# Stores of h issued by ScalarE, a fourth raw weight buffer, and no accumulating DMA in the first four down passes, in a two-layer encoder trunk on one core

## The chip, the core and the metric

The kernel runs on one NeuronCore of a Trainium2 chip. Its engines work from queues of their own, each in order: TensorE (PE; PEld is its loading of stationary weights), VectorE (DVE), ScalarE (ACT), GpSimd (POOL) and SyncE (SP, which here only issues DMAs). The metric is the time of one execution on the device in microseconds (us). The median of three runs of the kernel before is 1787.04 us.

## What is computed

A trunk of two layers on 768 tokens of width 1024 (512 of one request, 256 of another; the weights are shared). All of it is float32.

```
for layer in 0, 1:
    h = rmsnorm(x, ln_mix)
    x = x + attention(h @ w_in) @ w_out      # layer 0: neighbourhood and grouped heads; layer 1: differential
    h = rmsnorm(x, ln_mlp[layer])
    x = x + square(relu(h @ w_up[layer])) @ w_down[layer]     # 1024 -> 4096 -> 1024
y = rmsnorm(x, ln_f)
```

The change touches the MLP, `square(relu(h @ w_up)) @ w_down`.

## The kernel before

**Number format.** TensorE multiplies values rounded to fp32r. To keep float32 accuracy every operand is split in two parts, hi (rounded) and lo (the rest), and every product is done as three matmuls, hi·hi, lo·hi and hi·lo. A weight therefore passes through three kinds of tile: `wraw` (as loaded by a DMA that SP issues, L84), `whi` and `wlo`. The split has two forms. `wsplit` (L86): ScalarE copies hi (L90), VectorE subtracts (L91, lo = raw − hi). `wsplit_acc` (L93): ScalarE copies hi (L95) and writes raw times −1, rounded like hi, into lo (L96), and POOL issues a DMA that reads the raw weights from memory a second time and adds them to lo (L97, "accumulating DMA").

**Stages of the MLP** (`mlp`, L1145), the same in both layers. The 4096 hidden features are done in groups. Four groups of 128 are done plainly (`up_plain`, `down`). The rest goes in pairs of groups through a Strassen-Winograd scheme: seven products in place of eight.

- Fourteen *up passes* (`up_fast`, L948). Each takes one weight matrix of 2 x 2 quarters and the tokens in two halves of 384 and does seven products, numbered 0 to 6 here, of 12 matmuls of 128 x 384 each: 0, 2, 4 and 6 add into the PSUM tile upx (X), 1 writes upy (Y), 3 and 5 write upz (Z). ScalarE and VectorE take the results out, square the positive part, and form the seven combinations that the down passes need, in a staging tile `hf` of seven parts (two such tiles). That tile is stored to DRAM as `h` (L998). The last two up passes keep plain values and store them in pieces (L1001).
- Fourteen *down passes* (`down_fast`, L1038), in the order of `PASSES`. Before a pass runs, `Forms.need` (L1017) loads the stored forms back (L1020) into `hf`, and ScalarE and VectorE split them into hi and lo (L1032, L1033). The seven products go to dnx, dny and dnz, and VectorE adds them to x (L1046).

**Weights of a pass** (`quarters`, L908). Two raw tiles A and B are loaded (L84). From them come four pairs of hi and lo: w1 (the quarters a11 and a12, used by products 0 and 1), w2 (products 3 and 4), w3 (products 2 and 5) and w4 (product 6). w2 comes from sums of quarters (L921). The hi and lo tiles have four slots each, so each of w1 to w4 has one slot from pass to pass: w1 of the next pass can be written only when product 1 (Y) of this pass has been done. Which quarters take the accumulating form is set by `acc`: (11,) in the up passes, that is the first half of w1; (11, 12) in the down passes, that is all of w1.

**Order.** The code is recorded and a scheduler sets the order of instructions on each engine ahead of time, by priority (the order of the code) and by its own estimate of when operands and buffers are free. So the number of buffers, and the engine that issues a DMA, move instructions on every engine. At run time each engine goes through its list in order.

Of the kernel before, what the change touches and what calls it, by code (L numbers as in the profile page):

```python
# [12 lines left out]
F32 = mybir.dt.float32  # L13
# [5 lines left out]
P = 128  # L19
# [4 lines left out]
NT = TS + TP  # L24
# [22 lines left out]
def kernel(ctx: ExitStack, tc: tile.TileContext, a: dict, y: bass.AP):  # L47
    nc = tc.nc
# [4 lines left out]
    rpool = ctx.enter_context(tc.tile_pool(name="rpool", bufs=1, side="right"))  # L53
# [23 lines left out]
    def wload(src, width, pieces=1):  # L77

        off = woff.get(src, 0)
        woff[src] = off + P * width  # L80
        raw = rpool.tile([P, 1024], F32, tag="wraw", name="wraw", bufs=3)[:, :width]
        view = a[src][off : off + P * width].rearrange("(p w) -> p w", w=width)
        w = width // pieces
        return raw, [lambda s=slice(i * w, (i + 1) * w): nc.sync.dma_start(raw[:, s], view[:, s]) for i in range(pieces)]  # L84
# [8 lines left out]
    def wsplit_acc(hi, lo, raw, src):  # L93

        nc.scalar.activation(hi, raw, AF.Copy)  # L95
        nc.scalar.activation(lo, raw, AF.Copy, scale=-1.0)  # L96
        nc.gpsimd.dma_start(lo, src, accum_op=ALU.add)  # L97

    def whilo(width):
        return (wpool.tile([P, 1024], F32R, tag="whi", name="whi", bufs=4)[:, :width],  # L100
                wpool.tile([P, 1024], F32R, tag="wlo", name="wlo", bufs=4)[:, :width])
# [801 lines left out]
    def staging(mp):  # L903
        return mp.tile([P, 7, NH], F32, tag="hf", name="hf", bufs=2)
# [3 lines left out]
    def quarters(src, n, mp, acc):  # L908

        off = woff[src]  # L910
        dA, dB = (a[src][o : o + P * 2 * n].rearrange("(p w) -> p w", w=2 * n) for o in (off, off + P * 2 * n))
        A, loads = wload(src, 2 * n)
        loads[0]()
        B, loads = wload(src, 2 * n)
        loads[0]()
        lh, rh = slice(0, n), slice(n, 2 * n)
        a22, a11, a12, a21 = A[:, lh], A[:, rh], B[:, lh], B[:, rh]
        S = mp.tile([P, 1024], F32, tag="ws", name="ws", bufs=1)[:, : 2 * n]
        w1, w2, w3, w4 = whilo(2 * n), whilo(2 * n), whilo(2 * n), whilo(n)
        two = lambda t: t.rearrange("p (a b) -> p a b", b=n)  # L920
        add = lambda out, u, v: nc.vector.tensor_tensor(out=out, in0=u, in1=v, op=ALU.add)  # L921

        def plain(w, c, q, raw, src):
            if q in acc:
                wsplit_acc(w[0][:, c], w[1][:, c], raw, src)
            else:
                wsplit(w[0][:, c], w[1][:, c], raw)

        plain(w1, lh, 11, a11, dA[:, rh])
        plain(w1, rh, 12, a12, dB[:, lh])  # L930

        add(two(S), two(A), a21[:, None, :].broadcast_to([P, 2, n]))
        add(a21, S[:, lh], a11)
        add(a12, a12, a21)
        wsplit(*w3, B)
        wsplit(*w2, S)
        plain(w4, lh, 22, a22, dA[:, lh])
        return (w1, 0), (w1, n), (w3, n), (w2, 0), (w2, n), (w3, 0), (w4, 0)
# [9 lines left out]
    def up_fast(xs, T, mp, forms=True):  # L948


        ws = quarters("w_up", 512, mp, (11,))
        ta, tb = slice(*EVEN[0]), slice(*EVEN[1])
        quarter = lambda k0, c: [[t[:, c] for t in xs[k0 + kk]] for kk in range(KH)]
        X, Y, Z = ps_tile("mm", "upx")[:, :NH], ps_tile("at", "upy")[:, :NH], ps_tile("at", "upz")[:, :NH]
        s5 = mp.tile([P, NH], F32, tag="st", name="s5", bufs=3)
        if forms:
            st = staging(mp)
            b11, b21, t2, t1, t3, b22, t4 = (st[:, i] for i in range(7))
            b12 = mp.tile([P, NH], F32, tag="st", name="b12", bufs=3)
        else:  # L960
            f = [mp.tile([P, NT], F32, tag=t, name="f", bufs=GF) for t in ("hh", "hl")]
            b11, b12, b21, b22 = (t[:, c] for t in f for c in (ta, tb))
        op = lambda out, u, v, o: nc.vector.tensor_tensor(out=out, in0=u, in1=v, op=o)  # L963
        copy = lambda out, ps: nc.scalar.activation(out, ps, AF.Copy)

        def relu2(out, src, sign=1.0):
            nc.scalar.activation(out, src, AF.Relu, scale=sign)
            nc.scalar.activation(out, out, AF.Square)

        less = lambda out, u, v: nc.vector.scalar_tensor_tensor(out=out, in0=u, scalar=-1.0, in1=v, op0=ALU.mult, op1=ALU.subtract)  # L970

        product(X, ws[0], quarter(0, ta), True, False)
        copy(b11, X)
        product(Y, ws[1], quarter(KH, ta), True, True)
        op(b11, Y, b11, ALU.add)
        relu2(b11, b11)
        product(X, ws[2], T[1], False, False)
        copy(b12, X)
        product(Z, ws[3], T[0], True, False)
        copy(s5, Z)  # L980
        product(X, ws[4], T[2], False, False)
        copy(b22, X)
        op(b22, b22, s5, ALU.add)
        relu2(b22, b22, -1.0)
        product(Z, ws[5], quarter(KH, tb), False, True)
        op(b12, Z, b12, ALU.add)
        nc.vector.scalar_tensor_tensor(out=b12, in0=b12, scalar=0.0, in1=b12, op0=ALU.max, op1=ALU.mult)
        if forms:
            op(st[:, 3:5], st[:, 0:6:5], b12[:, None, :].broadcast_to([P, 2, NH]), ALU.subtract)
            less(t2, t3, b11)  # L990
        product(X, ws[6], quarter(0, tb), False, True)
        relu2(b21, X, -1.0)
        if forms:
            less(t4, t2, b21)
        kept = dram.tile([P, 7 if forms else 4, NH], F32, name=f"h{len(store)}")
        store.append(kept)
        if forms:
            nc.sync.dma_start(kept, st)  # L998
        else:
            for i, t in enumerate(f):  # L1000
                nc.sync.dma_start(kept[:, 2 * i : 2 * i + 2].rearrange("p a b -> p (a b)"), t)  # L1001
        return kept

    store = []
# [30 lines left out]
                    j += n  # L1035
                self.f.append(fs)

    def down_fast(x, p, fs, mp):  # L1038

        ws = quarters("w_down", len(fs) * P, mp, (11, 12))  # L1040
        ta, tb = slice(*EVEN[0]), slice(*EVEN[1])
        x0, x1 = x[2 * p], x[2 * p + 1]
        X, Y, Z = ps_tile("mm", "dnx")[:, :NH], ps_tile("at", "dny")[:, :NH], ps_tile("at", "dnz")[:, :NH]

        def onto(xm, c, ps, op=ALU.add):
            nc.vector.tensor_tensor(out=xm[:, c], in0=xm[:, c], in1=ps, op=op)  # L1046

        form = lambda i: [f[i] for f in fs]
        product(X, ws[0], form(0), True, False)
        onto(x0, ta, X)  # L1050
        product(Y, ws[1], form(1), True, True)
        onto(x0, ta, Y)
        product(X, ws[2], form(2), False, False)
        onto(x0, tb, X)
        product(Z, ws[3], form(3), True, False)
        onto(x1, tb, Z, ALU.subtract)
        product(X, ws[4], form(4), False, False)
        onto(x1, tb, X, ALU.subtract)
        product(Z, ws[5], form(5), False, True)
        onto(x0, tb, Z)  # L1060
        product(X, ws[6], form(6), False, True)
        onto(x1, ta, X, ALU.subtract)
# [82 lines left out]
    def mlp(layer, x, state, mp):  # L1145
        xs, T, second_half, sums, last_sum, first = state
        hs = up_plain(xs, mp, *first, second_half)
        with tc.high_priority(offset=-LATER):
            sums()
        down(hs, x, True)  # L1150
        last_sum()
        forms = Forms([up_fast(xs, T, mp) for _ in range(NU)], mp)
        rest = [up_fast(xs, T, mp, False) for _ in range(GF // 2)]
        for p, k0, k1 in PASSES:
            forms.need(k1)
            down_fast(x, p, forms.f[k0:k1], mp)
            if (p, k1) == (3, NU):
                hs = last_group(rest, mp)
        if layer == 1:
            return final(hs, x, lambda: xpool.tile([P, NT], F32, tag="xl", name="sq", bufs=8))  # L1160
        nxt, nn = [], Norm(lambda: mp.tile([P, NT], F32, tag="sq", name="sq", bufs=1))

        def ready(m):
            nxt.append(split(x[m], "x", gcol(G_O, m)))
            nn.add(x[m])

        down(hs, x, True, ready)
        return nxt, nn


    o, x, es = even_attention()
    es.close()
    ms = ExitStack()
    mp = ms.enter_context(tc.tile_pool(name="mlp0", bufs=2, side="left"))
# [8 lines left out]
    o, x, es = odd_attention(xs, nm, sg, spill)  # L1183
    es.close()
    mp = ctx.enter_context(tc.tile_pool(name="mlp1", bufs=2, side="left"))
# [140 lines left out]
```

## Time and profile before

| | |
|---|---|
| runs | 1783.54, 1787.04, 1790.44 us, median 1787.04 |
| profiled execution | 1786.56 us, its span 1784.8 us |
| busy | TensorE 1733.3, VectorE 1267.9, ScalarE 946.9, POOL 248.4 us |
| mean granted TensorE clock | 0.991 |
| up passes, layer 0 and layer 1 | from 447 to 651 us, and from about 1345 to 1550 us |
| a full up pass | 84 matmuls, about 14.56 us |

The span is the time from the first to the last instruction; busy times are of the span. An instruction's row in the profile carries its line in the code, the tile it writes and the tiles it reads, with buffer numbers left out, so `wlo<-wraw` is any of the low tiles. "A <- B" in a list of waits says that A was idle until B ended. A DMA's landing is counted from its issue.

### The profile page before, as it was taken

The page shows a single profiled execution, that of the slowest core. Times are in us where ns is not written, and L with a number is a line of the kernel's source. Part 1 is how long each engine was busy: PE and PEld are TensorE (multiplying, and loading weights), DVE is VectorE, ACT ScalarE, POOL GpSimd, SP SyncE. Part 2 cuts the span into 40 slices and gives each one's busy share as a digit, 9 for nine tenths or more (in the row PEclk, how much of TensorE's full clock was granted, in tenths as well). Part 3 has the DMA queues.
Part 4 walks back from the last instruction along what each step waited for, and adds up shares of the span by engine and source line. Part 5 has one row for each costly group of instructions (what it writes and reads, how often), then busy time and mean ns, then how long its engine had stood idle before and what let it go on. Part 6 is the DMA issues. An engine that isn't in the chain of part 4 may idle for free.

```text
span 1784.8 us, 28991 instructions
## 1 busy us (share of the span) xinstructions
PE 1733.3 (97%) x11098; PEld 1645.2 (92%) x11098; DVE 1267.9 (71%) x2458; ACT 946.9 (53%) x1981; POOL 248.4 (14%) x330
## 2 busy tenths in 40 slices
PE   7999999999999989999999999999999999989998
PEld 7878888899999989999999999988899999989997
DVE  7877646479566668886566767676696666688875
ACT  6765544344566665453435555554455666655534
POOL 3421000020000001111221312220200000011111
PEclk9999999999999999999999999999999999999999
DMA  5111222312565676764411101112124666777542
GB/s 166 48 34 40 65 86 90 124 34 66 143 188 183 213 251 177 234 172 99 153 48 48 48 25 46 54 57 95 36 66 132 184 186 186 244 216 230 157 102 83
DMA packets 61546, 214.49 MB, mean 120 GB/s; under 512 B 7136, under 2 KB 12512, under 8 KB 55264
## 3 DMA queue, kind: packets, MB, share of 16 engines
q1 hardware_dynamic: 47296, 190.08, 32.1%
q0 software_dynamic: 12096, 19.93, 7.1%
q10 hardware_dynamic: 2016, 2.64, 0.5%
q8 instruction: 87, 1.43, 0.3%
q14 instruction: 51, 0.42, 0.1%
HBM read 169.37 MB, written 42.47 MB: 119 GB/s over the span
## 4 chain that ended last, share of the span: by engine, by line
PE 84%; DVE 6%; DMA 4%; ACT 2%; issue 2%; POOL 1%; POOLq 0%; SPq 0%; DVEq 0%; ACTq 0%
PE upx L945 13%; PE dnx L945 9%; PE dqk L209 8%; PE upz L945 6%; PE dnz L945 4%; PE dvp L209 4%; PE upc L880 4%; PE opa L222 4%; PE upy L945 3%; PE dna L222 3%; PE dnb L222 3%; PE npa L222 2%; PE dny L945 2%; PE ds L288 2%; PE dpv L731 2%
## 5 line engine op out<-in xcount | busy, mean ns | idle before, releaser
L91 DVE TENSOR_TENSOR wlo<-wraw,whi 128x1024 fp32r<-128x1024 f32 (+3 forms) x232 | 224.3, 967 | 140.0 <-ACT whi L90 139.6
L90 ACT ACTIVATE whi<-wraw 128x1024 fp32r<-128x1024 f32 (+3 forms) x228 | 193.6, 849 | 177.8 <-PE dnx L945 70.5
L209 PE MATMUL dqk<-whi,xh 128*128 128x256 f32 x384 | 115.6, 301 | 0.0
L209 PE MATMUL dqk<-whi,xl 128*128 128x256 f32 x384 | 108.6, 283 | 0.0
L209 PE MATMUL dqk<-wlo,xh 128*128 128x256 f32 x384 | 108.4, 282 | 0.0
L716 ACT ACTIVATE de<-ds,m 128x512 f32<-128x512 f32 (+1 forms) x96 | 58.3, 612 | 79.7 <-DVE m L714 79.6
L97 POOL DMA_DIRECT2D wlo<-in_w_down_dram x56 | 49.3, 913 | 364.3 <-ACT wlo L96 277.3
L95 ACT ACTIVATE whi<-wraw 128x512 fp32r<-128x512 f32 (+3 forms) x84 | 49.2, 586 | 91.4 <-PE upy L945 36.6
L97 POOL DMA_DIRECT2D wlo<-in_w_up_dram x28 | 24.7, 883 | 452.6 <-DVE hf L963 301.1
L1046 DVE TENSOR_TENSOR x<-x,dnx 128x384 f32<-128x384 f32 x112 | 61.6, 550 | 33.9 <-PE dnx L945 33.1
L209 PEld LDWEIGHTS dqk<-whi,xh 128*128 128x128 f32 x384 | 73.1, 190 | 8.5 <-issue 7.7
L945 PE MATMUL upx<-Th,whi 128*128 128x384 f32 x224 | 74.9, 335 | 0.0
L945 PE MATMUL upx<-Th,wlo 128*128 128x384 f32 x224 | 74.8, 334 | 0.0
L945 PE MATMUL upx<-Tl,whi 128*128 128x384 f32 x224 | 74.8, 334 | 0.0
L945 PE MATMUL upx<-xh,whi 128*128 128x384 f32 x224 | 74.8, 334 | 0.0
L945 PE MATMUL upx<-xl,whi 128*128 128x384 f32 x224 | 74.8, 334 | 0.0
L945 PE MATMUL upx<-xh,wlo 128*128 128x384 f32 x224 | 74.8, 334 | 0.0
L90 ACT ACTIVATE whi<-ws 128x1024 fp32r<-128x1024 f32 (+3 forms) x56 | 56.0, 999 | 35.3 <-PE dnz L945 17.1
L209 PEld LDWEIGHTS dqk<-wlo,xh 128*128 128x128 f32 x384 | 73.3, 191 | 0.0
L209 PEld LDWEIGHTS dqk<-whi,xl 128*128 128x128 f32 x384 | 73.1, 190 | 0.0
L921 DVE TENSOR_TENSOR ws<-wraw 128x1024 f32<-128x1024 f32 (+3 forms) x56 | 64.1, 1145 | 11.3 <-DMA wraw<-in_w_down_dram 7.9
L158 POOL TENSOR_TENSOR acc<-acc,sq 128x384 f32<-128x384 f32 (+2 forms) x28 | 39.0, 1394 | 233.4 <-ACT sq L153 232.6
(350 smaller groups left out, 6103.0 us busy)
## 6 DMA issues: line engine op xcount, KB each, us to landing
wraw<-in_w_up_dram SPq DMA_DIRECT2D x64, 512.0 KB, 3.6
h<-hf SPq DMA_DIRECT2D x24, 1344.0 KB, 5.1
hf<-h SPq DMA_DIRECT2D x24, 1344.0 KB, 7.6
wraw<-in_w_down_dram SPq DMA_DIRECT2D x56, 512.0 KB, 3.8
wraw<-in_w_in_o_dram SPq DMA_DIRECT2D x24, 512.0 KB, 3.7
wlo<-in_w_down_dram POOLq DMA_DIRECT2D x40, 256.0 KB, 5.0
wraw<-in_w_in_e_dram SPq DMA_DIRECT2D x16, 512.0 KB, 3.7
wlo<-in_w_up_dram POOLq DMA_DIRECT2D x28, 256.0 KB, 6.0
```

What stands on the lines that cost most here:

```text
L90: nc.scalar.activation(hi, raw, AF.Copy)
L91: nc.vector.tensor_tensor(out=lo, in0=raw, in1=hi.bitcast(F32), op=ALU.subtract)
L95: nc.scalar.activation(hi, raw, AF.Copy)
L97: nc.gpsimd.dma_start(lo, src, accum_op=ALU.add)
L158: eng.tensor_tensor(out=self.acc[:, s], in0=self.acc[:, s], in1=sq, op=ALU.add)
L209: nc.tensor.matmul(ps[:, :256], st[:, tk], col(k, part, 0, 256), start=(k == 0 and i == 0), stop=(k == KD - 1 and i == 2))
L222: nc.tensor.matmul(ps[:, : e - s], lhs(k, part), mv[:, s:e], start=(k == 0 and i == 0), stop=(k == nk - 1 and i == 2))
L716: nc.scalar.activation(e, s, AF.Exp, bias=m, scale=1.0, accum_out=l2[:, c : c + 1])
L880: last = nc.tensor.matmul(ps, lhs(f0 + f, k, part), mv[:, s:e], start=(n == 0 and j == 0), stop=(n == KD - 1 and j == 2))
L921: add = lambda out, u, v: nc.vector.tensor_tensor(out=out, in0=u, in1=v, op=ALU.add)
L945: nc.tensor.matmul(ps, w[part][:, c], mv, start=(start and kk == 0 and j == 0), stop=(stop and kk == len(form) - 1 and j == 2), skip_group ...
L1046: nc.vector.tensor_tensor(out=xm[:, c], in0=xm[:, c], in1=ps, op=op)
```

## The change

```diff
-        raw = rpool.tile([P, 1024], F32, tag="wraw", name="wraw", bufs=3)[:, :width]
+        raw = rpool.tile([P, 1024], F32, tag="wraw", name="wraw", bufs=4)[:, :width]
...
         if forms:
-            nc.sync.dma_start(kept, st)
+            nc.scalar.dma_start(kept, st)
         else:
             for i, t in enumerate(f):
-                nc.sync.dma_start(kept[:, 2 * i : 2 * i + 2].rearrange("p a b -> p (a b)"), t)
+                nc.scalar.dma_start(kept[:, 2 * i : 2 * i + 2].rearrange("p a b -> p (a b)"), t)
...
-    def down_fast(x, p, fs, mp):
+    def down_fast(x, p, fs, mp, acc):
 
-        ws = quarters("w_down", len(fs) * P, mp, (11, 12))
+        ws = quarters("w_down", len(fs) * P, mp, acc)
...
-            down_fast(x, p, forms.f[k0:k1], mp)
+            down_fast(x, p, forms.f[k0:k1], mp, (11, 12) if k0 else ())
...
-        nxt, nn = [], Norm(lambda: mp.tile([P, NT], F32, tag="sq", name="sq", bufs=1))
+        nxt, nn = [], Norm(lambda: staging(mp)[:, 0:2].rearrange("p a b -> p (a b)"))
```

The raw weights get a fourth buffer. The stores of h (L998, L1001) are issued by ScalarE, not by SP. The four down passes that begin with the first form (k0 = 0, the first four of `PASSES`) split all of w1 with ScalarE and VectorE. The squares of layer 0's last norm go into a staging tile, which frees the room for the raw buffer.

The scheduler makes another order from it. TensorE in an up pass in the middle of layer 0: `upx_6203`, `upy_6204`, `upz_6205` are X, Y and Z of one pass, `upx_6339` is X of the next, whose w1 is `whi_6317` and `wlo_6318`. Before, behind the end of product 3:

```order
L945 MATMUL upz_6205<-Th_4606,whi_6183 128x384
L945 MATMUL upz_6205<-Tl_4607,whi_6183 128x384
L945 MATMUL upz_6205<-Th_4606,wlo_6184 128x384
L945 MATMUL upx_6203<-Th_4612,whi_6183 128x384
L945 MATMUL upx_6203<-Tl_4613,whi_6183 128x384
L945 MATMUL upx_6203<-Th_4612,wlo_6184 128x384
```

And now:

```order
L945 MATMUL upz_6205<-Th_4606,whi_6183 128x384
L945 MATMUL upz_6205<-Tl_4607,whi_6183 128x384
L945 MATMUL upz_6205<-Th_4606,wlo_6184 128x384
L945 MATMUL upx_6339<-xh_4533,whi_6317 128x384
L945 MATMUL upx_6339<-xl_4534,whi_6317 128x384
L945 MATMUL upx_6339<-xh_4533,wlo_6318 128x384
```

Product 0 of the next pass (and five matmuls of its Y) now stands ahead of products 4, 5 and 6 of this one; Y of this pass ends two products, 24 matmuls, ahead of it. In the pass that follows, product 0 of the one after stands ahead of products 5 and 6 only, three products behind the end of Y. The two kinds alternate.

ScalarE at the same place. Before:

```order
L964 ACTIVATE hf_6207<-upx_6203 128x384
L95 ACTIVATE whi_6317<-wraw_6312 128x512
L96 ACTIVATE wlo_6318<-wraw_6312 128x512
L90 ACTIVATE whi_6317<-wraw_6314 128x512
L967 ACTIVATE hf_6207<-hf_6207 128x384
L968 ACTIVATE hf_6207<-hf_6207 128x384
```

And now:

```order
L968 ACTIVATE hf_6071<-hf_6071 128x384
L95 ACTIVATE whi_6317<-wraw_6312 128x512
L96 ACTIVATE wlo_6318<-wraw_6312 128x512
L90 ACTIVATE whi_6317<-wraw_6314 128x512
L967 ACTIVATE hf_6207<-hf_6207 128x384
L998 DMA h6_6174<-hf_6071 128x2688
L968 ACTIVATE hf_6207<-hf_6207 128x384
```

L95 still waits for the last matmuls of Y of this pass, whose slot it writes, and the store of the pass before stands four instructions behind it. In passes of the other kind L90 stands between L95 and L96:

```order
L95 ACTIVATE whi_6181<-wraw_6176 128x512
L90 ACTIVATE whi_6181<-wraw_6178 128x512
L96 ACTIVATE wlo_6182<-wraw_6176 128x512
L964 ACTIVATE b12_6072<-upx_6067 128x384
L967 ACTIVATE hf_6071<-hf_6071 128x384
L998 DMA h5_6038<-hf_5935 128x2688
```

There the store stands behind a copy (L964) that waits for product 2.

VectorE where the down passes begin (layer 0; `f_7021` belongs to the last up pass, `wlo_7164` is the low part of w1 of the first down pass, `Tl` the low parts of combinations of a stored form). Before:

```order
L1033 TENSOR_TENSOR hl_7135<-hf_7124,hh_7134 128x768
L987 SCALAR_TENSOR_TENSOR f_7021<-f_7021 128x384
L921 TENSOR_TENSOR wraw_7160<-wraw_7160 128x256
L1046 TENSOR_TENSOR x1_3717<-x1_3717,dnx_7186 128x384
L91 TENSOR_TENSOR wlo_7168<-wraw_7160,whi_7167 128x512
```

And now:

```order
L1033 TENSOR_TENSOR hl_7135<-hf_7124,hh_7134 128x768
L987 SCALAR_TENSOR_TENSOR f_7021<-f_7021 128x384
L1033 TENSOR_TENSOR Tl_7147<-hf_7142,Th_7146 128x768
L1033 TENSOR_TENSOR Tl_7151<-hf_7142,Th_7150 128x768
L1033 TENSOR_TENSOR Tl_7155<-hf_7142,Th_7154 128x768
L91 TENSOR_TENSOR wlo_7164<-wraw_7158,whi_7163 128x256
L91 TENSOR_TENSOR wlo_7164<-wraw_7160,whi_7163 128x256
L921 TENSOR_TENSOR wraw_7160<-wraw_7160 128x256
L1046 TENSOR_TENSOR x1_3717<-x1_3717,dnx_7184 128x384
```

The three subtractions of the second form and two for w1's low part (L91) now stand between L987, the last but one step of the last up pass, and the first down result.

## The prediction

> **What bounds the kernel now.** I read the page first (busy time, the 40 slices, the chain of waits), then the windows, then TensorE's waits.
>
> ```profile
> PE 1733.3 (97%) x11098; PEld 1645.2 (92%) x11098; DVE 1267.9 (71%) x2458; ACT 946.9 (53%) x1981; POOL 248.4 (14%) x330
> PE 84%; DVE 6%; DMA 4%; ACT 2%; issue 2%; POOL 1%; POOLq 0%; SPq 0%; DVEq 0%; ACTq 0%
> 450.00:640.00 190.00, 190.00 (x1098) 190.00 (x1097) 125.51 (x179) 117.39 (x210) 11.33 (x13) 1.00 0.63 193
> ```
>
> TensorE (PE) is busy 97% of the span and carries 84% of the chain. The third line is a window (length, then PE, weight loads, VectorE, ScalarE, POOL, granted clock, DMA share, GB/s) over the thirteen up passes of layer 0 that follow its first products: PE idles for nothing in 190 us. An up pass has nothing to give; it can only lose. What TensorE waits for in the whole span, the largest rows that the change touches:
>
> ```profile
> PE dnx L945 <- DMA wlo<-in_w_down_dram: 10.9, 4, 3.2
> PE dnx L945 <- ACT whi L90: 4.1, 2, 2.1
> PE dny L945 <- DMA wlo<-in_w_down_dram: 2.5, 1, 2.5
> ```
>
> All lie where up passes end and down passes begin, once in each layer. The first and third, 10.9 + 2.5 = 13.4 us, are waits for the accumulating DMA.
>
> **Part 1: the fourth raw buffer changes TensorE's order.** Program text alone would say "loads come earlier". The order shown above says more: the first product of the next up pass now stands ahead of this pass's last two or three. That product needs the low part of w1, which is made in this sequence: the pass before must have finished its product Y (w1 has one set of slots, and Y is its last reader), then ScalarE copies hi (L95) and −raw (L96), POOL issues the accumulating transfer (L97), and it lands. Before, 62 matmuls stood between the end of Y and the first matmul that reads w1's low part. Counted in the changed order it is 26 in six of a layer's twelve steps from up pass to up pass, and 38 in the other six; in both layers. The sequence for one pass, before (start, length, instruction; in brackets the idle time ahead of it and what ended that):
>
> ```profile
> 611.13 0.33 PE L945 MATMUL upy<-xh,wlo 128*128 128x384 f32 x1
> 611.31 0.33 PE L945 MATMUL upx<-Th,whi 128*128 128x384 f32 x1
> 611.33 0.63 ACT L95 ACTIVATE whi<-wraw 128x512 fp32r<-128x512 f32 x1 [1.41 <-PE upy L945]
> 611.87 0.61 ACT L96 ACTIVATE wlo<-wraw 128x512 fp32r<-128x512 f32 x1
> 612.10 0.33 SPq L998 DMA_DIRECT2D h<-hf  x1
> 612.39 0.61 ACT L90 ACTIVATE whi<-wraw 128x512 fp32r<-128x512 f32 x1
> 612.91 0.51 ACT L967 ACTIVATE hf<-hf 128x384 f32<-128x384 f32 x1
> 612.84 0.88 POOL L97 DMA_DIRECT2D wlo<-in_w_up_dram  x1 [13.69 <-DVE hf L963]
> 619.79 4.16 PE upx L945 x24
> ```
>
> From the first matmul behind Y (611.31) to POOL's issue are 1.53 us. The landing, issue to landing, over the thirteen up passes:
>
> ```profile
> DMA to landing us min/median/max: 4.1/6.1/6.5
> wlo<-in_w_up_dram POOLq DMA_DIRECT2D x1, 256.0 KB, 4.1
> wlo<-in_w_up_dram POOLq DMA_DIRECT2D x1, 256.0 KB, 5.2
> 627.40 0.87 POOL L97 DMA_DIRECT2D wlo<-in_w_up_dram  x1 [13.69 <-ACT wlo L96]
> 625.59 0.33 SPq L998 DMA_DIRECT2D h<-hf  x1
> h<-hf SPq DMA_DIRECT2D x1, 1344.0 KB, 5.2
> wlo<-in_w_down_dram POOLq DMA_DIRECT2D x1, 256.0 KB, 3.8
> 646.95 7.36 DMA wlo<-in_w_down_dram
> ```
>
> The 4.1 is the first pass, with no store of h beside it; 5.2 the last, whose store was issued 1.8 us ahead (625.59 to 627.40); all others have a 1,344 KB store issued 0.74 us ahead (612.10) and take 5.8 to 6.5. In the changed order ScalarE issues that store about 0.5 us after POOL's issue: L90 and L967 (612.39 and 612.91 here) stand between L96 and the store. So both transfers still run together, and I take the median, 6.1: the low part is there 1.53 + 6.1 = 7.63 us after the matmul behind Y. A matmul takes 4.16 / 24 = 0.1733 us; 26 of them last 4.51 us, 38 last 6.59. Before, 62 lasted 10.75: 3.1 us to spare. Now TensorE stops for 7.63 − 4.51 = 3.12 us in the first kind. In the second kind ScalarE's order is L95, L90, L96, so POOL issues 0.52 us later: 8.15 − 6.59 = 1.56. TensorE takes matmuls in order, so products 4, 5 and 6 of the old pass, which are ready, queue behind that wait, and the up passes have no other idle time into which it could fall. Per layer 6 x (3.12 + 1.56) = 28.1 us, for both **+56.2**. Bounds: at 4.1 (nothing beside it) 12 x 1.12 = 13.4, with nothing in the second kind; at 7.36 (the slowest quoted) 12 x (4.38 + 2.82) = 86.4. 6.1 is nearest, being the same transfer beside the same store.
>
> That TensorE does stop when such a gap is short, this trace shows in the down passes. In the second one w1's slots come free 36 matmuls ahead of its first low-part matmul, and:
>
> ```profile
> 657.70 7.80 DMA wlo<-in_w_down_dram
> 665.55 0.44 PE L945 MATMUL dnx<-hh,wlo 128*128 128x384 f32 x1 [3.00 <-DMA wlo<-in_w_down_dram]
> ```
>
> **Part 2: the clock after a stop.** The other two stops of 3 us, and windows of 5 us in layer 0 (three) and layer 1 (two); the third number from the end is the granted clock:
>
> ```profile
> 654.35 0.44 PE L945 MATMUL dnx<-hh,wlo 128*128 128x384 f32 x1 [3.02 <-DMA wlo<-in_w_down_dram]
> 1552.91 0.44 PE L945 MATMUL dnx<-hh,wlo 128*128 128x384 f32 x1 [3.19 <-DMA wlo<-in_w_down_dram]
> 665.00:670.00 5.00, 3.77 (x14) 3.26 (x14) 1.67 (x4) 1.27 (x2) 0.00 (x0) 0.69 0.89 318
> 670.00:675.00 5.00, 3.64 (x11) 3.37 (x12) 4.79 (x7) 4.53 (x8) 0.87 (x1) 0.50 0.26 97
> 675.00:680.00 5.00, 5.00 (x25) 5.00 (x24) 3.08 (x5) 2.26 (x4) 0.87 (x1) 0.79 0.94 193
> 1555.00:1560.00 5.00, 5.00 (x22) 5.00 (x22) 4.23 (x9) 1.89 (x5) 0.87 (x1) 0.72 0.78 280
> 1580.00:1585.00 5.00, 2.48 (x15) 2.17 (x14) 3.28 (x6) 1.01 (x3) 0.00 (x0) 1.00 0.88 265
> ```
>
> The granted clock fell to 0.69, 0.50, 0.79 and 0.72 behind stops of about 3 us, and stayed 1.00 around the one of 2.5 us in the last row. Lost busy time: 3.77 x 0.31 + 3.64 x 0.50 + 5 x 0.21 + 5 x 0.28 = 5.4 us, over the five waits for the DMA and the two for ScalarE in the rows above, 0.8 each. I charge the twelve long new stops 0.8 each, **+9.6**, the short ones nothing; bounds 0 (none dips) and 12 x 1.8 = 22 (5.4 over three stops of 3 us or more). [...]
>
> **Part 3: no accumulating DMA in the first four down passes.** Removed there: eight L96 copies and eight POOL issues a layer. Added: eight VectorE subtractions a layer, two each of 256 and 384 columns, four of 512.
>
> ```profile
> 613.04 0.69 DVE L91 TENSOR_TENSOR wlo<-wraw,whi 128x512 fp32r<-128x512 f32 x1 [0.50 <-ACT whi L90]
> 644.34 2.81 DVE L1033 TENSOR_TENSOR Tl<-hf,Th 128x768 fp32r<-128x768 f32 x3 [0.55 <-ACT Th L1032]
> 650.60 0.55 DVE L987 SCALAR_TENSOR_TENSOR f<-f 128x384 f32<-128x384 f32 x1
> 651.07 0.42 DVE L921 TENSOR_TENSOR wraw<-wraw 128x256 f32<-128x256 f32 x1
> 663.05 0.55 DVE L1033 TENSOR_TENSOR xl<-hf,xh 128x384 fp32r<-128x384 f32 x1
> 680.00:685.00 5.00, 5.00 (x31) 5.00 (x30) 5.00 (x9) 2.53 (x3) 0.00 (x0) 1.00 0.84 259
> ```
>
> VectorE's price goes by width: 0.42, 0.55 and 0.69 us for 256, 384 and 512 columns, together 2 x 0.42 + 2 x 0.55 + 4 x 0.69 = 4.7 us a layer, on an engine that in 680 to 685 is busy all 5 us. And they stand late in its order: for the first down pass behind L987 (650.60) and three subtractions of 768 columns that used to be done by 647: 651.07 + 2.8 + 0.4 = 654.3, against 654.31 for the landing now (646.95 + 7.36). That stop stays. For the second pass they stand behind the 384-column L1033 of 663.05: first one done at about 664.0, against 665.5 now, 1.5 us gained. The stop for whi in that pass hangs on VectorE's order and stays, about a microsecond earlier; later ones shrink. I take 4 us a layer, **−8**. Bounds: −23 (13.4 of DMA waits, 4.1 for whi and 5.4 of clock all gone), +9.4 (all added subtractions on the chain); nearer the middle, since VectorE takes over the place of the DMA.
>
> **Part 4: hidden.** A store of h costs ScalarE one issue:
>
> ```profile
> L1127 ACTq DMA_DIRECT2D out_dram<-x x8: 338/338/354, 1770.9 to 1781.0; - x8
> 855.00:900.00 45.00, 45.00 (x326) 45.00 (x325) 22.12 (x35) 18.19 (x24) 9.14 (x7) 1.00 0.41 132
> ```
>
> The 12 stores of forms (L998) and 4 of plain h (L1001) leave SP's queue for ScalarE's: 16 x 0.34 = 5.4 us a layer on an engine busy 117 of 190 us in the up passes; it waits for a VectorE result of the pass before, done by then. If that cover went, L964's copies, which free TensorE's banks, would be late by 0.34 a pass. Stores no longer hold SP's queue, so raw loads leave a pass earlier; in the up passes they were in time already. The norm's squares, now in staging buffers (layer 0), are the same instructions, under products that keep PE busy 45.0 of 45 us; without that cover one of 768 columns would cost about a microsecond.
>
> **Sum**, against the profiled execution's own 1786.56 (0.5 below the median of the runs, 1787.04): 1786.6 + 56.2 + 9.6 − 8 = 1844.
>
> **Rivals.**
> 1. The transfer lands late: beside raw loads that now leave just behind the pass's last split, as in the 7.36 row. 1786.6 + 86.4 + 15 − 8 = 1880.
> 2. The transfer lands early, 4.1 us: 1786.6 + 13.4 − 8 = 1792, which can't be told from no change (under 0.5%, 9 us, a measurement of this kernel tells nothing). For it: the store starts behind it now. Against: it then overlaps all of it, before only its tail.
> 3. Faster: low parts in time everywhere. It takes a landing within 4.51 − 1.53 = 2.98 us of the issue; then Part 1 and 2 fall away, and Part 3 pays 8 to 23: 1764 to 1779. Against: no row is under 3.8 us. [...] The trace's 4.1 for a transfer with no store beside it speaks against it.
>
> **How the numbers follow.** Forecast (landing 5 to 6.8 us) 0.72, late 0.12, early 0.10, faster 0.06. Predicted 1844. Range 1800 to 1872: from a landing of 4.6 (1786.6 + 20.2 + 0 − 6) to 6.5 with every long stop dipping (1786.6 + 65.8 + 22 − 2), leaving out rivals 1, most of 2, and 3. Faster 0.05, within 0.5% 0.10, slower 0.85.
>
> **What would show it.** Right: in the profile after, TensorE's wait list has a new first row, upx waiting for the DMA of wlo from w_up, 24 times, some 56 us, longest near 3; TensorE's busy share in 450 to 640 falls from all to about 85%; granted clock under 1 in the up slices. Part 3: the dnx waits for that DMA vanish, and waits for VectorE's wlo (L91) stand there. Wrong: no upx wait, which would mean landings under 3 us; or a wait of ScalarE at L998 for VectorE, which I took as nothing.

## The result, and the profile after

The changed kernel takes 1879.6 us (median, 1873.18 to 1886.14) against 1788.2 for the kernel before: 1.0515 times as long, 95% interval [1.0468, 1.0562]. The profiled execution has a span of 1871.1 us, 86.3 more than the 1784.8 of before. Forecast was 1844, within 1800 to 1872: the direction was right, the size too small. One of the four runs of experiment 6 below ran at a lower clock (0.842 in place of 0.981 to 0.986; 1928.95 us) and is left out of its time.

The page's busy line and chain of waits, and the window over the up passes of layer 0 (columns as before):

```profile
PE 1762.9 (94%) x11098; PEld 1671.9 (89%) x11098; DVE 1275.4 (68%) x2474; ACT 935.9 (50%) x1965; POOL 234.3 (13%) x314
PE 73%; DVE 9%; DMA 9%; issue 4%; ACT 3%; POOL 1%; DVEq 0%; POOLq 0%; SPq 0%; ACTq 0%
450.00:640.00 190.00, 164.16 (x881) 161.27 (x880) 102.17 (x145) 93.83 (x170) 9.58 (x11) 0.93 0.48 145
```

In the window, TensorE's busy time fell from all of it to 164 of 190 us, and the granted clock from 1.00 to 0.93. TensorE's 11,098 matmuls are the same; busy time grew by 30 us, as each takes longer where the granted clock is down (behind the stop shown below, at 0.50, they start 0.32 us apart, before it 0.17). TensorE's waits:

```profile
PE upx L945 <- DMA wlo<-in_w_up_dram: 64.2, 21, 4.3
PE dnx L945 <- DVE wlo L91: 9.6, 5, 2.9
PE dnx L945 <- ACT whi L90: 1.8, 2, 1.5
```

The first row is new, and is TensorE's largest wait. Its waits of dnx and dny for the accumulating DMA (10.9 and 2.5 us before) are gone from the list; L91 stands in their place. One step from pass to pass, of the kind with 26 matmuls between:

```profile
607.25 0.33 PE L945 MATMUL upy<-xh,wlo 128*128 128x384 f32 x1
607.42 0.34 PE L945 MATMUL upx<-Th,whi 128*128 128x384 f32 x1
607.44 0.63 ACT L95 ACTIVATE whi<-wraw 128x512 fp32r<-128x512 f32 x1 [0.16 <-PE upy L945]
607.98 0.61 ACT L96 ACTIVATE wlo<-wraw 128x512 fp32r<-128x512 f32 x1
608.95 0.87 POOL L97 DMA_DIRECT2D wlo<-in_w_up_dram  x1 [14.49 <-DVE hf L970]
608.99 0.33 ACTq L998 DMA_DIRECT2D h<-hf  x1
609.03 0.51 ACT L967 ACTIVATE hf<-hf 128x384 f32<-128x384 f32 x1
wlo<-in_w_up_dram POOLq DMA_DIRECT2D x1, 256.0 KB, 7.3
616.27 0.69 PE L945 MATMUL upx<-xh,wlo 128*128 128x384 f32 x1 [4.17 <-DMA wlo<-in_w_up_dram]
```

The first matmul behind Y starts at 607.42; POOL issues 1.53 us later, as forecast. ScalarE issues the store of h 0.04 us behind that, not 0.5: in its order the store stands behind the copy of L967, but it leaves 0.04 us before that copy starts. The transfer lands after 7.3 us, not 6.1, and TensorE stops for 4.17 us. Its first matmul then takes 0.69 us, twice the usual 0.33, with the granted clock at 0.50. Windows of 5 us over the same place (third number from the end: granted clock):

```profile
605.00:610.00 5.00, 5.00 (x30) 5.00 (x30) 4.81 (x8) 4.06 (x9) 0.87 (x1) 1.00 0.25 78
610.00:615.00 5.00, 2.09 (x13) 1.77 (x11) 2.36 (x3) 0.96 (x3) 0.00 (x0) 0.93 1.01 342
615.00:620.00 5.00, 3.73 (x12) 3.74 (x13) 0.00 (x0) 0.13 (x1) 0.00 (x0) 0.50 0.07 12
620.00:625.00 5.00, 5.00 (x28) 5.00 (x27) 0.63 (x1) 1.80 (x3) 0.00 (x0) 0.89 0.00 0
```

Where the 86 us lie. "Up" is the time from the first start of a matmul that writes upx to the last in that layer, "down" from there to the last of dnx. In layer 0 after, the first and last up matmul and the first down matmul are:

```profile
445.57 0.34 PE L945 MATMUL upx<-xh,whi 128*128 128x384 f32 x1
695.53 0.33 PE L945 MATMUL upx<-xh,wlo 128*128 128x384 f32 x1
695.70 0.33 PE L945 MATMUL dnx<-hh,whi 128*128 128x384 f32 x1
```

| us | up, layer 0 / 1 | down, layer 0 / 1 |
|---|---|---|
| before | 203.7 / 203.8 | 192.9 / 192.0 |
| after | 250.0 / 256.3 | 185.4 / 187.6 |

By the unrounded starts the up passes lost 98.7 us and the down passes gained 12.0; the difference, 86.8, is the span's 86.3 but for half a microsecond.

### The profile page after: what moved, and what is told of

Same layout as the page of the kernel before. It is cut to its first block, busy times and chain, and to the rows that moved or that the text cites. A ratio compares the mean times of both kernels' runs of the same rounds, so it can differ in the third digit from the quotient of the medians.

```text
span 1871.1 us, 28950 instructions
## 1 busy us (share of the span) xinstructions
PE 1762.9 (94%) x11098; PEld 1671.9 (89%) x11098; DVE 1275.4 (68%) x2474; ACT 935.9 (50%) x1965; POOL 234.3 (13%) x314
## 4 chain that ended last, share of the span: by engine, by line
PE 73%; DVE 9%; DMA 9%; issue 4%; ACT 3%; POOL 1%; DVEq 0%; POOLq 0%; SPq 0%; ACTq 0%
PE dnx L945 11%; DMA wlo<-in_w_up_dram 7%; PE dqk L209 7%; PE upx L945 6%; PE dnz L945 5%; PE dvp L209 4%; PE upc L880 4%; PE opa L222 4%; PE dna L222 3%; PE dnb L222 3%; PE dny L945 3%; PE npa L222 2%; PE upz L945 2%; DVE wlo L91 2%; PE ds L288 2%
## 5 line engine op out<-in xcount | busy, mean ns | idle before, releaser
L91 DVE TENSOR_TENSOR wlo<-wraw,whi 128x1024 fp32r<-128x1024 f32 (+4 forms) x248 | 232.9, 942 | 157.6 <-ACT whi L90 157.1
L90 ACT ACTIVATE whi<-wraw 128x1024 fp32r<-128x1024 f32 (+4 forms) x244 | 200.7, 828 | 189.1 <-PE dnx L945 63.1
L945 PE MATMUL upx<-xh,wlo 128*128 128x384 f32 x224 | 86.4, 388 | 64.3 <-DMA wlo<-in_w_up_dram 64.2
L945 PEld LDWEIGHTS upx<-xh,wlo 128*128 128x128 f32 x224 | 48.5, 217 | 71.3 <-DMA wlo<-in_w_up_dram 71.3
L964 ACT ACTIVATE hf<-upx 128x384 f32<-128x384 f32 x48 | 23.3, 485 | 129.4 <-PE upx L945 113.3
L945 PE MATMUL upx<-xl,whi 128*128 128x384 f32 x224 | 82.7, 369 | 0.0
L945 PE MATMUL upx<-xh,whi 128*128 128x384 f32 x224 | 82.6, 369 | 0.0
L97 POOL DMA_DIRECT2D wlo<-in_w_down_dram x40 | 35.2, 910 | 365.5 <-ACT wlo L96 177.8
L90 ACT ACTIVATE whi<-ws 128x1024 fp32r<-128x1024 f32 (+3 forms) x56 | 55.9, 998 | 36.7 <-PE upz L945 20.9
L95 ACT ACTIVATE whi<-wraw 128x512 fp32r<-128x512 f32 (+2 forms) x68 | 40.4, 594 | 54.7 <-PE dny L945 26.2
```

The lines of the kernel that those rows point to most:

```text
L91: nc.vector.tensor_tensor(out=lo, in0=raw, in1=hi.bitcast(F32), op=ALU.subtract)
L945: nc.tensor.matmul(ps, w[part][:, c], mv, start=(start and kk == 0 and j == 0), stop=(stop and kk == len(form) - 1 and j == 2), skip_group ...
```

## The experiments

The theory of the prediction: a stop in each step from up pass to up pass, since the accumulating transfer lands later than the matmuls between last. Its rivals: another part of the change than the one named, the raw loads, or the new order of TensorE by itself. Runs 1, 2, 4, 5 and 10 take the three parts apart; the others change the transfer, or what runs beside it.

**1. Stores alone.** The kernel before, with

```
-            nc.sync.dma_start(kept, st)
+            nc.scalar.dma_start(kept, st)
```

and the same for the plain stores.

> The kernel before with one part of the change alone: ScalarE issues the stores of h (L998, L1001); three raw buffers, all accumulating DMAs kept. The order of TensorE in the up passes is that of the changed kernel (26 and 38 matmuls between the end of Y and the first matmul that reads w1's low part, 62 before). Theory A, the stores' change of engine is what brings the new order and with it the stops: up passes 45 to 55 us a layer longer than before, TensorE's wait of upx for the low part 55 to 70 us, time 1870 to 1895 us, a little over the changed kernel, since the down passes gain nothing. Rival B, as the prediction has it, the fourth raw buffer is the cause (through earlier raw loads beside the accumulating transfers): 1780 to 1800 us.

Measured: 1878.15 us, ratio 1.0509 [1.0484, 1.0534]; up 237.9 / 239.6, down 202.5 / 202.8. Its waits:

```profile
PE upx L945 <- DMA wlo<-in_w_up_dram: 44.6, 12, 4.0
PE dnx L945 <- DMA wlo<-in_w_down_dram: 27.8, 4, 9.7
PE dny L945 <- DMA wlo<-in_w_down_dram: 5.8, 4, 2.3
```

Theory A: the stores alone bring the new order, and as much time as the whole change. It comes in another way, though. Only the twelve steps of 26 matmuls stop (44.6 us, below the 55 to 70 expected; the up passes are 34 and 36 us longer, not 45 to 55), and the down passes, expected to gain nothing, lose 10 us a layer. The two plain stores (L1001) that ScalarE issues leave 0.3 and 1.4 us behind the first accumulating transfer there, where before they left 4.2 and 5.1 us behind it; that transfer lands after 10.6 us, not 7.4, and TensorE waits up to 9.7 us for it. A second load of a form now leaves 2.7 us behind it as well, and which of the two delays it more is not shown.

**2. The change without its stores** (the fence above, undone).

> The changed kernel with the stores of h back on SP's queue; the fourth raw buffer, the norm's squares in a staging tile and the plain splits of the first four down passes stay. TensorE's order in the up passes is that of before (62 matmuls). Theory A (the stores bring the stops): up passes 204 us each as before, no wait of upx for the low part, and the down passes' gain remains, about 6 us a layer: 1770 to 1782 us, faster than before. Rival B (the fourth raw buffer brings the stops): 1860 us or more. Rival C (the down passes gain nothing by themselves): 1783 to 1792.

Measured: 1767.11 us, ratio 0.9889 [0.9861, 0.9917]; up 203.7 / 203.8, down 181.8 / 183.2. Below the expected 1770. Over the up passes of layer 0:

```profile
450.00:640.00 190.00, 190.00 (x1098) 190.00 (x1097) 125.02 (x181) 118.45 (x213) 11.35 (x13) 1.00 0.62 192
```

TensorE is busy throughout again, at a granted clock of 1.00. So moving the stores is what costs, and the rest of the change is a gain: this kernel beats both.

**3. The change, with w1 split plainly in the up passes too.**

```
-        ws = quarters("w_up", 512, mp, (11,))
+        ws = quarters("w_up", 512, mp, ())
```

> The changed kernel with one thing added: in the up passes, too, the first half of w1 is split by ScalarE and VectorE, so no accumulating DMA is left there. The order of TensorE is that of the changed kernel (26 and 38). Theory A (TensorE stops because the accumulating transfer takes 6 to 7 us to land, and 26 or 38 matmuls, 4.5 or 6.6 us, don't cover it): the low part is there some 1.5 to 2.5 us behind Y, all stops in the up passes go, the clock stays 1.00, and the 0.69 us of VectorE a pass is hidden: 1768 to 1785 us. Rival B (the new order itself costs, whatever makes the low part): stops of 1 to 3 us stay, now for L91, 1800 to 1860 us.

Measured: 1773.38 us, ratio 0.9931 [0.9905, 0.9958]; up 203.7 / 203.7, down 184.0 / 185.5.

```profile
450.00:640.00 190.00, 190.00 (x1098) 190.00 (x1097) 132.25 (x190) 109.42 (x196) 0.00 (x0) 1.00 0.48 174
```

Beside the row of experiment 2, in the same window: in the up passes TensorE's new order costs nothing, and neither do ScalarE's stores as such. With the accumulating transfer gone (POOL 0.00) there is no stop, and VectorE's 7 us more are hidden. The transfer's landing is the cause of the stops. The down passes are 4.5 us longer than in experiment 2; what of ScalarE's stores does that is not shown.

**4. Plain splits in the first four down passes alone.** The kernel before with `down_fast(x, p, forms.f[k0:k1], mp, (11, 12) if k0 else ())`.

> The kernel before with the second part of the change alone: the first four down passes split all of w1 with ScalarE and VectorE. Three raw buffers, stores on SP, TensorE's order in the up passes as before. Theory A (the prediction's Part 3): the waits of dnx and dny for the accumulating DMA, 13.4 us, go, waits for L91 of 5 to 10 us take their place, and 4 to 6 us a layer are gained: 1774 to 1781 us. Rival B (VectorE takes as long as the DMA did): within 0.3% of before, 1782 to 1792 us.

Measured: 1770.16 us, ratio 0.9908 [0.9887, 0.9928]; down 182.5 / 183.2.

```profile
PE dnx L945 <- DVE wlo L91: 3.2, 2, 1.6
PE dnx L945 <- ACT whi L90: 2.9, 2, 1.5
```

More than expected, and twice the prediction's 8 us: the down passes are shorter by (192.9 + 192.0) − (182.5 + 183.2) = 19.2 us.

**5. Fourth raw buffer alone** (`bufs=4`, and the squares in a staging tile).

> The kernel before with the third part of the change alone: a fourth raw weight buffer, and the room for it (layer 0's squares in a staging tile). Stores on SP, all accumulating DMAs kept, TensorE's order in the up passes as before. Theory A (the buffer changes nothing that TensorE waits for): no stop in the up passes, time 1780 to 1792 us, within 0.5% of before. Rival B (raw loads that leave earlier run beside the accumulating transfers, land them late and bring stops): longer than 1800 us.

Measured: 1787.17 us, ratio 0.9997 [0.9979, 1.0015]; up 203.7 / 203.7. Theory A. The transfer in the up passes is later all the same (layer 0; before it was 4.1/6.1/6.5):

```profile
DMA to landing us min/median/max: 4.1/6.9/7.0
```

The store still leaves 0.7 to 0.9 us ahead of POOL's issue; new beside it is a 512 KB raw load 2.3 us ahead. The 62 matmuls of cover hide the 0.8 us.

**6. A fifth slot for low parts** (`name="wlo", bufs=5`; three raw buffers).

> The changed kernel with five slots for low parts (wlo) in place of four, and three raw buffers, to make room. TensorE's order stays that of the changed kernel. The low part of the next w1 now has a slot of its own, so ScalarE's copy (L96) no longer waits for the end of Y: in the order it stands ahead of L95, behind a copy of product 0. Theory A (the chain that stops TensorE begins when Y frees w1's slot): POOL issues about 2 us earlier in the steps with 26 matmuls, stops fall from 4 to about 2 us there and vanish in the others, 12 x 2.1 = 25 us in all. By the clock of the runs so far (stops of 1.2 to 1.4 us lost 0.27 us beside themselves, those of 2.5 us and more 1.6 to 3.3) a stop of 2 us is not known: if the clock holds, 1786 + 25 + 3 - 12 = 1802 us; if it falls behind each, about 1825. Rival B (the start doesn't matter, the transfer lands when the store lets it): stops stay near 4 us, 1850 us or more.

Measured: 1825.8 us, ratio 1.0209 [1.0174, 1.0244]; up 227.2 / 229.2.

```profile
PE upx L945 <- DMA wlo<-in_w_up_dram: 31.3, 10, 3.8
494.51 0.33 PE L945 MATMUL upy<-xh,wlo 128*128 128x384 f32 x1
494.91 0.87 POOL L97 DMA_DIRECT2D wlo<-in_w_up_dram  x1 [13.52 <-PE upy L945]
wlo<-in_w_up_dram POOLq DMA_DIRECT2D x1, 256.0 KB, 7.6
```

The start matters: POOL issues 0.40 us behind the start of Y's last matmul, against 608.95 − 607.25 = 1.70 in the changed kernel. But the transfer took longer still (7.6 here, 7.1 to 8.2 in these steps), so the stops are 3.1 us, not 2.1, and there are ten, not twelve. The time agrees with the branch in which the clock falls (1825) partly by luck: the stops come to 31 us in place of 25, the rest of the up passes' loss to 18 in place of some 26.

**7. Half the transfer.**

```
+            if q in acc and half:
+                m = raw.shape[-1] // 2
+                e, g = slice(c.start, c.start + m), slice(c.start + m, c.stop)
+                wsplit_acc(w[0][:, e], w[1][:, e], raw[:, :m], src[:, :m])
+                wsplit(w[0][:, g], w[1][:, g], raw[:, m:])
```

> The changed kernel with half the accumulating transfer in the up passes: 256 of the 512 columns of the first half of w1 come by the accumulating DMA (128 KB in place of 256), the other 256 are split by ScalarE and VectorE. Stores on ScalarE and four raw buffers as in the changed kernel; TensorE's order nearly so (26 and 38 matmuls, one step more of 26 at the start of a layer). Theory A (the landing goes by the bytes of the transfer): it lands in 4 to 5 us, POOL issues 0.3 us earlier, stops of 0.7 to 1.7 us, little clock lost: 1795 to 1815 us. Rival B (the landing is set by the 1,344 KB store and the raw loads beside it, whatever the size): still 6.5 to 7.5 us, stops of about 3.5 us with the clock down behind them: 1850 to 1880 us.

Measured: 1847.7 us, ratio 1.0318 [1.0276, 1.0361]; up 238.2 / 242.4. A pass with no store beside it, and one with the store 0.36 us behind:

```profile
wlo<-in_w_up_dram POOLq DMA_DIRECT2D x1, 128.0 KB, 3.1
523.62 0.87 POOL L97 DMA_DIRECT2D wlo<-in_w_up_dram  x1 [12.86 <-DVE hf L968]
523.98 0.33 ACTq L1003 DMA_DIRECT2D h<-hf  x1
wlo<-in_w_up_dram POOLq DMA_DIRECT2D x1, 128.0 KB, 7.2
```

Where the store starts 0.3 to 0.5 us behind, half the bytes land nearly as late as all of them (6.0 to 7.2 us), and 1.0 us earlier (3.1 against 4.1) where none is there: rival B, for the passes in which the store starts with it. The time lies just under B's range: in the passes where the store starts 1.4 us behind, it landed after 4.5 to 5.4 us, but for one of 7.0.

**8. Stores on SP, no accumulating DMA in any down pass** (`down_fast(..., ())`).

> The changed kernel with the stores back on SP's queue, and with no accumulating DMA in any of the fourteen down passes of a layer. Theory A (the gain of the plain split lies in the four passes in which the trunk turns from up to down, where TensorE waited; later passes have 62 matmuls of cover): no further gain over the kernel with stores on SP and four plain passes (1767 us): 1764 to 1772. Rival B (later landings also cost): 1755 to 1763. Rival C (VectorE, with ten more passes of subtractions, becomes late): 1775 to 1800.

Measured: 1766.14 us, ratio 0.9876 [0.9845, 0.9907]; down 180.7 / 183.3. Theory A: nothing beyond the first four passes that can be told from experiment 2.

**9. A short store.**

```
-            nc.scalar.dma_start(kept, st)
+            nc.scalar.dma_start(kept[:, :1], st[:, :1])
```

and loads that read that part seven times.

> The changed kernel with a store of one part of the seven in place of all (192 KB in place of 1,344 KB, still issued by ScalarE); the loads of the down passes read that part seven times, so six parts of each form are left out and the numbers of the MLP are not the reference's. With so short a store the order of TensorE is that of before (62 matmuls), so no stop is expected in any case and the time is 1755 to 1770 us, near the kernel with stores on SP; the run is for the landing of the accumulating transfer in the up passes. Theory A (the 1,344 KB store that starts beside it makes it late): 4.1 to 4.8 us in all up passes, as where no store stands beside it. Rival B (the raw loads beside it, or the transfer's place behind the engine's other work): 5.5 to 7 us as in the changed kernel.

Measured: 1773.64 us in one run, a little above the expected range, beside 1790.56 for the kernel before. Landings in layer 0:

```profile
504.52 0.33 SPq L84 DMA_DIRECT2D wraw<-in_w_up_dram  x1
506.79 0.86 POOL L97 DMA_DIRECT2D wlo<-in_w_up_dram  x1 [13.70 <-DVE hf L963]
508.02 0.33 ACTq L998 DMA_DIRECT2D h<-hf  x1
DMA to landing us min/median/max: 4.0/4.1/10.7
```

In eleven of thirteen passes 4.0 to 4.2 us, though a raw load leaves 2.3 us ahead; the other two (10.7 and 6.5) have a 1,344 KB load of a form (L1020) beside them, and the first of these brings a stop of 1.33 us that was not expected. So a raw load 2.3 us ahead does not delay the transfer by itself, and the 1,344 KB store does, as theory A says.

**10. The change with three raw buffers** (`bufs=3`).

> The changed kernel with three raw weight buffers, as before; stores on ScalarE and the plain splits of the first four down passes stay. TensorE's order is that of the changed kernel. The kernel with the stores alone (three buffers) has up passes of 238 and 240 us and stops only in the steps with 26 matmuls; the changed kernel has 250 and 256 us and stops in both kinds. Theory A (the fourth buffer lets raw loads leave beside the accumulating transfers of the steps with 38 matmuls and lands those late): up passes of 237 to 241 us a layer, about 12 stops, and with the changed kernel's down passes 1840 to 1855 us. Rival B (the fourth buffer has no part in it, the difference lies in the store's start, which the plain splits moved): up passes stay at 248 us or more, 1865 to 1885 us.

Measured: 1846.11 us, ratio 1.0329 [1.0309, 1.035]; up 238.7 / 238.9, down 188.0 / 187.9.

```profile
PE upx L945 <- DMA wlo<-in_w_up_dram: 43.7, 12, 4.0
```

Theory A. The fourth buffer costs nothing with SP's stores, and some 33 us with ScalarE's (1879.6 − 1846.1). A step of 38 matmuls in the changed kernel, and the same kind of step with three buffers (experiment 1):

```profile
630.78 0.33 SPq L84 DMA_DIRECT2D wraw<-in_w_up_dram  x1
630.93 0.88 POOL L97 DMA_DIRECT2D wlo<-in_w_up_dram  x1 [21.10 <-DVE wlo L91]
632.19 0.33 ACTq L998 DMA_DIRECT2D h<-hf  x1
wlo<-in_w_up_dram POOLq DMA_DIRECT2D x1, 256.0 KB, 8.2
626.85 0.33 SPq L84 DMA_DIRECT2D wraw<-in_w_up_dram  x1
628.43 0.88 POOL L97 DMA_DIRECT2D wlo<-in_w_up_dram  x1 [19.24 <-DVE hf L963]
630.26 0.33 ACTq L998 DMA_DIRECT2D h<-hf  x1
wlo<-in_w_up_dram POOLq DMA_DIRECT2D x1, 256.0 KB, 4.4
```

With four buffers the raw load leaves 0.15 us ahead of POOL's issue and the store 1.26 us behind it; with three, 1.58 ahead and 1.83 behind, and there is no stop. In the changed kernel these steps land between 4.0 and 8.4 us. The raw load's shift alone is enough for the landings of 5.4 to 5.8 us: in experiment 6 four transfers have no store beside them and a raw load within 0.3 us of their issue, and they land after 5.4 to 6.0 us. What tells the 8 us ones from those of 5.7, which have the same neighbours, stays open.

## Why the prediction was right in kind and wrong in size

The profiled execution took 1873.2 us, some 29 more than the sum of the prediction: the clock's term is 24.9 us short, the stops' 8.0, and Part 3 gained 4.0 more than forecast.

- **Part 1, the mechanism: right.** TensorE's new order leaves 26 or 38 matmuls to cover the making of w1's low part; TensorE stops for the accumulating transfer, with the rest of the old pass queued behind. The 1.53 us from Y to POOL's issue, the 4.51 us of cover, and the waits' place were as forecast. Experiment 3 takes the transfer away and the stops go with it.
- **Part 1, the name: wrong.** The prediction put the new order down to the fourth raw buffer. Experiments 1, 2, 5 and 10 show that the stores' change of engine brings it, with three buffers or four, and that the buffer alone brings no stop. What the buffer did was to bring eight of the twelve steps of 38 matmuls to a stop of 0.8 us or more (a ninth stops for 0.16), with raw loads leaving just ahead of the transfer, somewhat as rival 1 had it, but only with ScalarE's stores.
- **Part 1, the size: somewhat too small.** 64.2 us in 21 stops, against 56.2 in 24. The step that failed is "I take the median, 6.1", as "the same transfer beside the same store". The stops of the first kind average 3.88 us (forecast 3.12), with landings of 6.7 to 7.3 in eleven of the twelve. There the store leaves between 0.8 us ahead of POOL's issue and 0.25 behind it, not 0.5 behind, and a 512 KB raw load leaves 1.4 to 2.3 us ahead, which Part 1's sum did not count. Experiment 5, with the store where it was, gives such a raw load, beside the store, 0.8 us (6.1 to 6.9); how the rest divides is not shown. The second kind averages 1.46 over its twelve steps (forecast 1.56), but as nothing or 0.16 in four, about 1.2 in five, and 3.8 to 4.0 in three: that the average fits is luck. The upper bound took 7.36 as the slowest landing, while the next fence of the prediction shows 7.80; the slowest here was 8.4.
- **Part 2, the clock: the term that was mis-sized most.** Forecast 9.6 us, bound 22; measured 98.7 − 64.2 = 34.5. The step that failed is "charge the twelve long new stops 0.8 each". It averaged the loss over seven stops of before, of which three alone were followed by a lower clock, and took it from busy time in windows, which leaves out the slow start behind every stop (a first matmul of 0.44 us or more in place of 0.33). Added up from matmul to matmul (each start less the one before, less the stop and the usual 0.1733 us), those seven lost 8.7 us, not 5.4. In the changed kernel the fifteen stops of 2.5 to 4.3 us cost 1.6 to 3.0 us each beside themselves, 2.2 on average, and the six shorter ones 0.3. The last section counts behind which idling the granted clock fell in these traces.
- **Part 3: right in sign, too small.** Forecast −8. In the changed kernel −12.0 (the down columns above), alone −19.2 in the down passes (experiment 4: 16 us of median). The prediction's first stop did stay after the change (2.36 us in layer 0, for L91), the second and third shrank to 1.82 and 1.46, from 3.00 and 2.05, and what was lost behind these two beside their length fell from 4.3 to 1.1 us (added up as in Part 2), though behind the first it rose from 0.6 to 1.9. That was not in the sum. In experiment 4, whose order differs again, the first stop is gone.
- **Part 4: the store is not hidden.** Its issue (0.33 us in the rows above) costs ScalarE nothing that matters (experiment 3), as said. But the place and the start of its transfer decide when the low part lands, and in experiment 1 it cost the down passes 20 us more. The plain splits of the change, which take the transfer off that place, spared the changed kernel most of this loss (its down passes are still 8.0 us longer than those of experiment 2): the parts can't be added up one by one.
- **The rivals.** The time is that of rival 1 (1880), not by its sum: it had 86.4 us of stops and 15 of clock (a figure that the prediction doesn't work out), the runs show 64.2 and 34.5. Rival 2 needs landings of 4.1 us; no step of the first kind had one under 5.7. What was held against it, that before the store overlapped "only its tail", is a misreading: the store left 0.74 us ahead and took 5.2, so it ran beside 4.5 of the transfer's 6.1 us. Rival 3 needs a landing within 2.98 us and is refuted: without a 1,344 KB transfer beside it, the 256 KB took 4.0 to 4.2 us in eleven passes of experiment 9.

## What to carry to other kernels

When a DMA issue moves to another engine, ask first what the scheduler makes of it on the engine that is the bound, and then what the transfer now starts beside: here a small transfer on the critical chain (256 KB) took 4.0 to 4.2 us with none of 1,344 KB beside it (eleven passes of experiment 9) and 6.7 to 7.3 beside one that starts at nearly the same moment (eleven of the twelve steps of 26 matmuls in the changed kernel), and half its size landed little sooner there (6.0 to 7.2, experiment 7). A stop of TensorE of 2.5 to 4.3 us cost 1.6 to 3.0 us more than its length in the changed kernel, so take the transfer off the chain (a plain split here, under VectorE's cover) or the start of the large one away from it, and price parts of a change together: the fourth buffer was free with one engine's stores, and cost some 33 us with the other's.

## What the runs showed of the hardware

The clock behind a stop. In the up passes of four kernels (after, experiments 1, 6 and 7) TensorE waited 62 times for this transfer. What each stop lost beside its own length, until the next, worked out from the matmuls' starts as above:

| length of the stop, us | stops | loss beside it over 1 us | range of that loss, us |
|---|---|---|---|
| up to 1.5 | 11 | 0 | 0.28 to 0.41 |
| 2.2 to 3.1 | 17 | 16 | 1.60 to 2.02, once 0.29 |
| 3.1 to 3.5 | 8 | 8 | 1.74 to 2.93 |
| 3.5 to 4.3 | 26 | 26 | 1.69 to 3.15 |

```profile
599.34 0.44 PE L945 MATMUL upx<-xh,wlo 128*128 128x384 f32 x1 [1.30 <-DMA wlo<-in_w_up_dram]
543.09 0.69 PE L945 MATMUL upx<-xh,wlo 128*128 128x384 f32 x1 [2.54 <-DMA wlo<-in_w_up_dram]
```

These two rows are of the changed kernel: behind 1.30 us of idling the first matmul takes 0.44 us, and 0.28 us are lost in all; behind 2.54 it takes 0.69, and 1.6 us are lost. Length alone does not decide, though. Experiment 6 has two stops of 2.98 us, of which the first lost 0.29 us and the second 1.85:

```profile
571.29 0.44 PE L945 MATMUL upx<-xh,wlo 128*128 128x384 f32 x1 [2.98 <-DMA wlo<-in_w_up_dram]
566.18:569.59 3.41, 2.14 (x13) 1.82 (x11) 1.52 (x3) 1.48 (x4) 0.00 (x0) 1.00 1.03 320
569.59:573.00 3.41, 1.71 (x10) 1.71 (x11) 0.00 (x0) 0.00 (x0) 0.00 (x0) 1.00 0.44 173
573.00:576.42 3.42, 3.42 (x21) 3.42 (x20) 0.00 (x0) 0.97 (x2) 0.00 (x0) 1.00 0.00 0
603.67 0.68 PE L945 MATMUL upx<-xh,wlo 128*128 128x384 f32 x1 [2.98 <-DMA wlo<-in_w_up_dram]
600.31:603.72 3.41, 0.43 (x4) 0.11 (x2) 0.00 (x0) 0.49 (x1) 0.00 (x0) 1.00 0.76 282
603.72:607.14 3.42, 3.42 (x11) 3.42 (x12) 0.00 (x0) 0.00 (x0) 0.00 (x0) 0.50 0.00 0
```

In each of the twelve traces the granted clock is 1.00 or 0.50 (a value between is the mean over a window), and all its changes lie a whole number of steps of 3.413 us apart; the windows are cut on these steps. In the changed kernel's trace, around the stop of 4.17 us that ends at 616.27:

```profile
607.43:610.84 3.41, 3.41 (x21) 3.41 (x21) 3.22 (x6) 2.99 (x6) 0.87 (x1) 1.00 0.62 220
610.84:614.25 3.41, 1.25 (x8) 0.93 (x6) 1.52 (x3) 0.49 (x1) 0.00 (x0) 1.00 1.00 352
614.25:617.67 3.42, 1.40 (x4) 1.41 (x5) 0.00 (x0) 0.00 (x0) 0.00 (x0) 0.50 0.33 62
617.67:621.08 3.41, 3.41 (x12) 3.41 (x12) 0.00 (x0) 0.49 (x1) 0.00 (x0) 0.50 0.00 0
621.08:624.49 3.41, 3.41 (x22) 3.41 (x21) 0.12 (x1) 1.21 (x2) 0.00 (x0) 1.00 0.00 0
```

The first stop of experiment 6 lies across the end of such a step, so TensorE idles 3.41 − 2.14 = 1.27 us in one step and 1.70 in the next, and the clock stays 1.00. The second lies within one step, which idles 2.98 us, and the next step runs at 0.50. Counted over the up and down passes of all twelve traces, 2,719 steps ran at 1.00. Behind the 82 that idled 1.95 us or more the next step was always at 0.50, behind the 2,622 that idled under 1.67 never, and behind the 15 in between seven times; what decides among those stays open. So what a stop cost in these traces went with its length and with where it fell: the 11 of up to 1.5 us lost 0.28 to 0.41 us, all 34 of more than 3.1 us lost 1.69 or more, and of the 17 between, one that was split over two steps lost 0.29. A step at half clock that PE fills costs, by an estimate from these records, half of 3.41, that is 1.7 us, and the clock stayed down for a second one where the first still idled 0.60 us or more.
